# An encoder layer on one core: the exponentials' table and the values' scaling moved to ScalarE behind a maximum, a rotation bound to group 1, and unit products ahead of the first projection

## Chip, core and metric

The kernel runs on 1 core of one Trainium2 chip. The time is device microseconds (us) of one execution, measured on that core. The engines are TensorE (PE for its matmuls, PEld for its weight loads), VectorE (DVE), ScalarE (ACT), GpSimd (POOL) and SyncE (SP, which only issues DMAs here).

## What is computed

One encoder layer with two mixers side by side, on 1024 tokens of width 1024, all in float32. The change touches the input projection and mixer A.

```python
def reference(x, norm1_g, w_in, qa_norm_g, ka_norm_g, ...):
    tables = axial_rope_tables(s)
    hn = rms_norm(x, norm1_g)
    proj = hn @ w_in                       # 1024 x 2304: qa 512, ka 128, va 128, qb 512, kb 512, vb 512
    ...
    qa = apply_axial_rope(rms_norm(qa, qa_norm_g), tables)   # 8 heads of 64
    ka = apply_axial_rope(rms_norm(ka, ka_norm_g), tables)   # 2 heads of 64
    out_a = global_gqa_attention(qa, ka, va)                 # dense softmax over 1024 keys
    out_b = dilated_mixture_attention(rms_norm(qb, qb_norm_g), rms_norm(kb, kb_norm_g), vb)
    mixed = jnp.concatenate([rms_norm(out_a, outa_norm_g), rms_norm(out_b, outb_norm_g)], axis=-1)
    x = x + mixed @ w_out
    return x + conv_ffn(rms_norm(x, norm2_g), w_up, conv_w, conv_b, w_down)
```

## The kernel before

**Arithmetic.** A float32 operand is kept as two parts, high and low, and a product is three matmuls (high x high, high x low, low x high). ACT makes the high part with a copy, DVE or POOL the low part with a subtraction (`split`, lines 231 to 233; `kv_split` for the key and value weights, 270 to 273).

**Stages.** Tokens come in 8 tiles of 128. First, tile by tile, `x_prep(tt)` transposes the tokens on PE (line 180) and splits them, `x_rest(tt)` takes the sum of squares for the norm on ACT (`Square`, line 248, with a read-out instruction) and copies the transposed tokens out of PSUM (line 252, and 254 to 258 for tiles 4 to 7), `kv_proj(tt)` computes keys and values of mixer A (lines 283 to 285, 24 matmuls), and `kv_out(tt)` copies them out (line 295) and sends them to memory. Then come 28 block products (`in_product`, lines 408 to 410; `in_out`, line 420, empties a product's bank on DVE), seven for each of four chunks kb, vb, qa, qb of the weights; `w_scale` (367) and `w_prep` (381 to 392) scale, combine and split the weights. The first products stand in the code between the tiles' projections.

**Around the last products.** `k_ready(u)` transposes the rotated keys and copies them to SBUF twice on ACT (336, 337). `v_scale` multiplies the values by the norm of their token on DVE (348). Line 1062 is an exponential of one element with scale 0, there to load the table of the exponentials on ACT. `load_v` (699) fetches values of mixer B from memory; `v_split` makes their high part on ACT (709).

**Mixer A** is 16 groups g: query tiles b = g // 2 and key head kv = g % 2. `a_prep(g)` makes the queries: split (613, 614), transposes and a copy on ACT (`first`, 629), four maxima over all keys (`mx`, two matmuls 634 and two DVE reductions 635 each) and `last` (638, 642). `a_main(g)` runs 8 key tiles: scores (661, 662), exponential on ACT (664), product with the values (656) two tiles later; beside them it takes the next group's `a_prep` by the table `plan` and deferred steps by the table `late_plan`. `o_norm` (681, 682) divides.

**Rotation.** Norm and rotation of the queries are lists of steps (`done`). Those of the last query product are not done at once but `deferred`: the steps from the third on of `deferred[0]` (query tiles 4 to 7, key head 1) and `deferred[1]` (the same tiles, key head 0) go into `late`. In them POOL multiplies by the sine part (`rot`, line 289, and 504), DVE by the cosine part and adds (511, 514). Query tiles 4 to 7 are read by the groups from 8 on.

**What sets the order.** The code is written once in program order; a scheduler of the framework then puts each engine's instructions in an order of its own, within the dependencies it sees, and sets the waits. An instruction can be held back by letting it read an element that another writes, or write one that another reads: a small copy with such operands is called a tick here. Each engine runs its instructions in order.

Of the kernel before, what the change touches and what calls it, by code (L numbers as in the profile page):

```python
# [43 lines left out]
R_K2A = 16384  # L44
# [79 lines left out]
def tile_encoder_layer(ctx, tc, x, w_in, gains, outg, norm1_g, norm2_g, w_out, w_up, conv_w, conv_b,  # L124
# [110 lines left out]
    def x_bank(tt):  # L235
        return 4 + 2 * (tt % 2)
# [8 lines left out]
    def x_rest(tt):  # L245
        q0, q1 = qab(tt % 4), qab(tt % 4 + 4)
        b = x_bank(tt), x_bank(tt) + 1
        act(f(F_JNK, 512).bitcast(BF), f(qab(tt), 1024), AF.Square, accum_out=f(SM_SS1 + tt, 1))
        vec.tensor_scalar(f(SM_E1 + tt, 1), f(SM_SS1 + tt, 1), EPS / D, EPS * EPS, op0=OP.mult, op1=OP.add)
        if tt < 4:  # L250
            for half in range(2):
                act(f(q0 + 512 * half, 512), bank(b[half]), AF.Copy)
        else:
            act(f(q1, 512), bank(b[0]), AF.Copy)
            vec.tensor_tensor(f(q1 + 512, 512), f(q0, 512), bank(b[0]), op=OP.subtract)
            vec.tensor_tensor(f(q1, 512), bank(b[1]), f(q1, 512), op=OP.add)
            gp.tensor_tensor(f(q0, 512), f(q1, 512), f(q0, 512), op=OP.subtract)
            gp.tensor_tensor(f(q0 + 512, 512), f(q0 + 512, 512), f(q0, 512), op=OP.subtract)
# [16 lines left out]
    def kv_bank(tt):  # L275
        return tt if tt < 4 else 2 + tt % 2

    def kv_proj(tt):
        for k in range(8):
            a = a_op(((1, 2), (3, 4))[tt // 4][k // 4], tt % 4) + 128 * (k % 4)  # L280
            w = R_A[7] + 2048 * (k // 4) + 256 * (k % 4)
            o = bank(kv_bank(tt), 256)
            mm(o, r(a, 128), r(w, 256), start=(k == 0), stop=False)
            mm(o, r(a, 128), r(w + 1024, 256), start=False, stop=False)
            mm(o, r(a + 512, 128), r(w, 256), start=False, stop=(k == 7))
# [57 lines left out]
                kvscr[:, :, 128 + 64 * kv:192 + 64 * kv].rearrange("t p c -> p t c"))  # L343

    def v_scale():
        for kv in range(2):
            v = fp(F_VA + 66 * kv, [132, 8], [1, 64])
            vec.tensor_tensor(v, v, f(SM_R1, 8)[:, :, None].to_broadcast([128, 8, 64]), op=OP.mult)

    def fill_k():  # L350
        for i in range(4):
# [210 lines left out]
    dma(f(qab(3), 1024), perm_rows(x, 3, D))  # L562
    w_load(0, 0)
    vec.tensor_copy(r(R_IDR, 128), f(O_IDF, 128))
    nc.tensor.transpose(bank(7, 8), f(F_CST, 128)[0:8], f(O_IDF, 8)[0:8])
    vec.tensor_copy(f(SM_G1, 8), bank(7, 8))
    x_prep(0)
    for k in range(8):
        kv_split(k)
    x_prep(1)  # L570
    dma(f(F_ROPE, 1024), rope)
    for i, o in enumerate((O_GA, O_GA + 128, O_GB, O_GB + 64)):
# [406 lines left out]

    prep = [lambda: fill(rp(R_QLN + 64, [128, 8], [1, 64]), 8, 64, 0.0, eng=act)] + a_prep(0)  # L980
    for i in range(4):
        kv_proj(i)
        x_rest(i)
        x_prep(i + 2)
        if i == 0:
            late_consts()
        kv_out(i)
        if i == 2:
            w_scale(0, 0)
            w_prep(0)  # L990
        if i == 3:
            w_scale(0, 1)
            w_prep(1)
    v, rt = f(SM_T + 96, 8), f(SM_MC + 8, 8)
    for m in range(len(prods)):
# [61 lines left out]
        if last and n == 7:  # L1057
            for u in (1, 2):
                k_ready(u)
            v_scale()  # L1060

            act(f(SM_T + 96, 1), rf(R_K2A + 512, 1), AF.Exp, scale=0.0)
        if last and n == 6:
            k_ready(3)
            take(prep, 3)
        if last and n == 3:
            take(prep, 3)
    take(prep, 99)
    assert not going
    deferred += later  # L1070
    late = last_sums + [t for d in deferred[:2] for t in done(*d, 0)[3:]]

    spread = {}
    for i, d in enumerate(deferred[2:]):
        square_at, mean_at, root_at, refine_at, norm_at, gain = done(*d, i)
        spread[5 + i, 2] = [square_at]
# [13 lines left out]
    for g in range(16):  # L1090

        prep += a_prep(g + 1) if g < 15 else []
        if g == 14:
            prep += [lambda: b_split(0)] + b_prep(0)
        tail = a_main(g, prep, tail, late, {14: (1, 1, 1, 1, 1, 2, 2, 2), 15: (2, 2, 2, 2, 1, 1, 1, 1)}.get(
            g, (1, 1, 1, 1, 1, 1, 1, 0)),
                      (0, 1, 1, 0, 1, 0, 1, 0) if g < 3 else (0, 0, 1, 0, 1, 0, 1, 0) if g < 7 else (0, 1, 0, 0, 0, 1, 0, 0))
        if g == 7:
            dma(f(F_CNT, 384), cnt)
            gp.memset(fp(F_VCN + 64, [66, 8]), 1.0)  # L1100
# [417 lines left out]
```

## Times and profile before

| | before |
|---|---|
| runs | 1340.53, 1342.11, 1344.23 us (median 1342.11) |
| profiled execution | 1342.88 us, span 1341.1 us |
| PE busy | 1310.6 us, 98% of the span |
| DVE, ACT, POOL busy | 987.8, 677.1, 361.1 us |
| mean granted PE clock | 0.998 |

PE is busy in nearly the whole span. So its idle time, and the few stretches in which its clock is granted at half, are what remains to look at; idle time of the other engines matters only where PE waits for them. In the rows below a time in brackets with an arrow is the idle time ahead of that instruction, and after the arrow stands what ended it.

### The profile page before, as it was taken

How to read it: one execution, taken by the hardware profiler on the slowest of the kernel's cores; microseconds unless marked ns; L12 is line 12 of the kernel's file. 1: busy time of each engine (PE TensorE's matmuls, PEld its weight loads, DVE VectorE, ACT ScalarE, POOL GpSimd, SP SyncE). 2: the span in 40 equal slices, each digit the busy share in tenths (PEclk: the TensorE clock that was granted, in tenths of full speed). 3: DMA queues.
4: the chain of work that ended last, by engine and by line, in shares of the span. 5: the costliest groups of instructions: out<-in, count | busy, mean ns of one | idle time of the engine just before them, and what ended most of it. 6: DMA issues, size and time to landing. Idle time of an engine off the chain costs nothing.

```text
span 1341.1 us, 20092 instructions
## 1 busy us (share of the span) xinstructions
PE 1310.6 (98%) x7559; PEld 1135.3 (85%) x7559; DVE 987.8 (74%) x1629; ACT 677.1 (50%) x1062; POOL 361.1 (27%) x274
## 2 busy tenths in 40 slices
PE   7999999999999999999999999999999999999998
PEld 7999999999999888878877788888888888888887
DVE  4987686455655888875578877887787789586664
ACT  7855563455545676764365444444444445244331
POOL 0611123000111221100014565556656651100000
PEclk9999999999999999999999999999999999999999
DMA  7145212000000243342222333232233325887973
GB/s 256 52 111 126 80 39 65 9 1 0 1 9 29 67 111 109 95 147 82 94 87 71 103 110 110 87 102 96 102 115 106 102 101 190 286 295 239 297 225 110
DMA packets 119859, 148.08 MB, mean 110 GB/s; under 512 B 50833, under 2 KB 76881, under 8 KB 119761
## 3 DMA queue, kind: packets, MB, share of 16 engines
q1 hardware_dynamic: 118609, 143.65, 33.3%
q0 software_dynamic: 1152, 3.15, 0.9%
q8 instruction: 59, 0.97, 0.3%
q14 instruction: 39, 0.32, 0.1%
HBM read 112.95 MB, written 33.82 MB: 109 GB/s over the span
## 4 chain that ended last, share of the span: by engine, by line
PE 73%; DVE 13%; ACT 6%; issue 3%; POOL 3%; DMA 1%; SPq 0%; ACTq 0%; DVEq 0%; POOLq 0%
PE ps L1223 8%; PE ps L1224 8%; PE ps L1225 8%; PE ps L656 7%; PE ps L1339 5%; PE ps L1340 5%; PE ps L1338 5%; PE ps L661 3%; PE ps L634 2%; DVE bigf L1256 2%; PE ps L662 2%; PE ps L837 2%; PE ps L904 2%; PE ps L906 2%; PE ps L905 2%
## 5 line engine op out<-in xcount | busy, mean ns | idle before, releaser
L1223 PE MATMUL ps<-bigr 128*128 128x512 f32 x616 | 241.1, 392 | 6.7 <-DVE bigf L1227 6.1
L1224 PE MATMUL ps<-bigr 128*128 128x512 f32 x616 | 239.7, 389 | 0.0
L1225 PE MATMUL ps<-bigr 128*128 128x512 f32 x616 | 239.7, 389 | 0.0
L1206 ACT ACTIVATE bigr<-bigf 128x512 fp32r<-128x512 f32 x154 | 92.9, 625 | 159.2 <-POOL bigf L1198 95.4
L1256 DVE SCALAR_TENSOR_TENSOR bigf<-bigf 128x768 f32<-128x768 f32 (+1 forms) x176 | 146.3, 889 | 26.3 <-ACT bigf L1254 26.3
L656 PEld LDWEIGHTS ps<-bigf 128*128 128x128 f32 x1024 | 139.4, 191 | 10.4
L1223 PEld LDWEIGHTS ps<-bigr 128*128 128x128 f32 x616 | 115.6, 188 | 35.8 <-DVE bigf L1227 9.9
L1318 ACT ACTIVATE bigr<-bigf 128x1024 fp32r<-128x1024 f32 x77 | 80.7, 1060 | 119.2 <-PE ps L1340 71.3
L1207 DVE TENSOR_TENSOR bigr<-bigf,bigr 128x512 fp32r<-128x512 f32 x112 | 116.6, 1058 | 32.6 <-ACT bigr L1206 32.6
L1225 PEld LDWEIGHTS ps<-bigr 128*128 128x128 f32 x616 | 115.6, 188 | 23.9
L1224 PEld LDWEIGHTS ps<-bigr 128*128 128x128 f32 x616 | 115.7, 188 | 23.7
L656 PE MATMUL ps<-bigf 128*128 128x65 f32 x1024 | 134.3, 267 | 0.0
L408 PE MATMUL ps<-bigr 128*128 128x256 f32 x448 | 127.7, 285 | 1.2 <-ACT bigf L295 1.2
L409 PE MATMUL ps<-bigr 128*128 128x256 f32 x448 | 127.3, 284 | 0.0
L410 PE MATMUL ps<-bigr 128*128 128x256 f32 x448 | 127.1, 284 | 0.0
L664 ACT ACTIVATE bigf<-ps 128x512 f32<-128x512 f32 x128 | 76.0, 597 | 92.6 <-PE ps L662 91.5
L1338 PE MATMUL ps<-bigr 128*128 128x512 f32 x308 | 119.8, 389 | 0.0
L1339 PE MATMUL ps<-bigr 128*128 128x512 f32 x308 | 119.8, 389 | 0.0
L1340 PE MATMUL ps<-bigr 128*128 128x512 f32 x308 | 119.8, 389 | 0.0
L1319 DVE TENSOR_TENSOR bigr<-bigf,bigr 128x1024 fp32r<-128x1024 f32 x77 | 93.0, 1221 | 26.6 <-ACT bigr L1318 22.4
L635 DVE TENSOR_REDUCE bigf<-ps 128x1 f32<-128x512 f32 x128 | 86.5, 690 | 22.8 <-PE ps L634 20.9
L1270 POOL TENSOR_TENSOR bigf<-bigf 128x512 f32<-128x512 f32 x44 | 69.1, 1591 | 89.9 <-DVE bigf L1261 65.6
(228 smaller groups left out, 2889.8 us busy)
## 6 DMA issues: line engine op xcount, KB each, us to landing
bigf<-w_down SPq DMA_DIRECT2D x99, 256.0 KB, 4.4
bigf<-w_up SPq DMA_DIRECT2D x44, 512.0 KB, 4.3
bigf<-gscr SPq DMA_DIRECT2D x77, 256.0 KB, 4.0
gscr<-bigf SPq DMA_DIRECT2D x33, 512.0 KB, 2.7
bigf<-w_in SPq DMA_DIRECT2D x8, 1024.0 KB, 5.4
bigf<-x SPq DMA_DIRECT2D x15, 512.0 KB, 6.9
bigf<-tmx SPq DMA_DIRECT2D x8, 672.0 KB, 3.7
bigf<-w_out SPq DMA_DIRECT2D x8, 512.0 KB, 5.9
```

The costliest lines, as they stand in the source:

```text
L408: mm(o, ah, wh, start=(k == 0 and t % 2 == 0 and n != 2), stop=False, skip_group_check=True)
L409: mm(o, ah, wl, start=False, stop=False, skip_group_check=True)
L410: mm(o, al, wh, start=False, stop=(k == 3), skip_group_check=True)
L656: mm(bank(ob, 65, 66 * i), f(slots[kt] + 128 * i, 128), f(F_VA + 132 * kt + 66 * kv, 65), start=(kt == 0 and i == 0), stop=(kt == 7), skip ...
L1207: (gp if n in (2, 4) and m > 3 else vec).tensor_tensor(rp(o + 512, [128, 4], [1, 128]), src, rfp(o, [128, 4], [1, 128]), op=OP.subtract)
L1223: mm(bank(b), wh, th, start=(k == 0 and n in (1, 5, 6, 7)), stop=False, skip_group_check=True)
L1224: mm(bank(b), wh, tl, start=False, stop=False, skip_group_check=True)
L1225: mm(bank(b), wl, th, start=False, stop=(k == 3), skip_group_check=True)
L1256: vec.scalar_tensor_tensor(f(a + o, n), f(i + d, n), w_, f(a + o, n), op0=OP.mult, op1=OP.add)
L1338: mm(o, ah, r(d, 512), start=(q == 0 and n in (1, 5, 2)), stop=False, skip_group_check=True)
L1339: mm(o, ah, r(d + 1024, 512), start=False, stop=False, skip_group_check=True)
L1340: mm(o, al, r(d, 512), start=False, stop=(q == NQ - 1), skip_group_check=True)
```

## The change

Four things. (1) In `v_scale` the two DVE multiplications become eight ACT copies with a scale per partition, behind two small DVE copies, of which the first reads a maximum; the one-element exponential that loads the table stands behind the first queries' copy, and `v_scale` behind the maxima. (2) The steps of `deferred[1]` from the third on (`turns`) leave `late` and are given to `spread` in group 1: three at key tile 2 behind a tick, two at key tile 4, the rest at key tile 7; `late_plan` is one table for all groups. (3) Ahead of the transposes of norm_g twelve products of the unit matrix with itself go to a bank that nobody reads; behind token tile 0 follow one that reads its second half, and sixteen more. The first half of the first key and value projection stands ahead of token tile 1. (4) In `x_rest` a tick, for all tiles but the first, lets the sum of squares wait for DVE's part of the split.

```diff
     def x_rest(tt):
         q0, q1 = qab(tt % 4), qab(tt % 4 + 4)
         b = x_bank(tt), x_bank(tt) + 1
+        if tt:
+
+            vec.tensor_copy(f(F_JNK, 1), rf(a_op(((1, 2), (3, 4))[tt // 4][1], tt % 4) + 512, 1))
         act(f(F_JNK, 512).bitcast(BF), f(qab(tt), 1024), AF.Square, accum_out=f(SM_SS1 + tt, 1))
...
-    def kv_proj(tt):
-        for k in range(8):
+    def kv_proj(tt, ks=range(8)):
+        for k in ks:
...
     def v_scale():
-        for kv in range(2):
-            v = fp(F_VA + 66 * kv, [132, 8], [1, 64])
-            vec.tensor_tensor(v, v, f(SM_R1, 8)[:, :, None].to_broadcast([128, 8, 64]), op=OP.mult)
+
+        vec.tensor_copy(f(SM_SS1, 1), f(SM_MC, 1))
+        vec.tensor_copy(f(SM_SS1, 8), f(SM_R1, 8))
+        for t in range(8):
+            v = fp(F_VA + 132 * t, [66, 2], [1, 64])
+            act(v, v, AF.Copy, scale=f(SM_SS1 + t, 1))
...
     vec.tensor_copy(r(R_IDR, 128), f(O_IDF, 128))
+
+    idle = lambda n: [mm(bank(0, 128), r(R_IDR, 128), r(R_IDR, 128), start=True, stop=True) for _ in range(n)]
+    idle(12)
     nc.tensor.transpose(bank(7, 8), f(F_CST, 128)[0:8], f(O_IDF, 8)[0:8])
     vec.tensor_copy(f(SM_G1, 8), bank(7, 8))
     x_prep(0)
+
+    mm(bank(0, 128), r(R_IDR, 128), r(a_op(2, 0), 128), start=True, stop=True)
+    idle(16)
     for k in range(8):
         kv_split(k)
+    kv_proj(0, range(4))
     x_prep(1)
...
-        kv_proj(i)
+        kv_proj(i, range(0 if i else 4, 8))
...
-            v_scale()
-
-            act(f(SM_T + 96, 1), rf(R_K2A + 512, 1), AF.Exp, scale=0.0)
         if last and n == 6:
             k_ready(3)
-            take(prep, 3)
+            take(prep, 1)
+
+            act(f(SM_T + 96, 1), rf(R_Q2A, 1), AF.Exp, scale=0.0)
+            take(prep, 2)
         if last and n == 3:
             take(prep, 3)
+            v_scale()
...
-    late = last_sums + [t for d in deferred[:2] for t in done(*d, 0)[3:]]
-
-    spread = {}
+    late = last_sums + done(*deferred[0], 0)[3:]
+    turns = done(*deferred[1], 0)[3:]
+
+    spread = {(1, 2): [lambda now: vec.tensor_copy(f(F_KN[0], 1), now)] + [lambda now, t=t: t() for t in turns[:3]],
+              (1, 4): [lambda now, t=t: t() for t in turns[3:5]], (1, 7): [lambda now, t=t: t() for t in turns[5:]]}
...
-                      (0, 1, 1, 0, 1, 0, 1, 0) if g < 3 else (0, 0, 1, 0, 1, 0, 1, 0) if g < 7 else (0, 1, 0, 0, 0, 1, 0, 0))
+                      (0, 2, 2, 2, 1, 1, 1, 1))
```

The changed kernel's lines are shifted: from `x_rest` on by 3, from `v_scale` on by 6, from the start's code on by 9 to 13.

PE's first rows of the order, before. L180 is a transpose of tokens, L565 that of norm_g, L283 to L285 the first key and value projection.

```order
L180 MATMUL ps<-bigf 128x128 x8
L565 MATMUL ps<-bigf 128x8
L283 MATMUL ps<-bigr 128x256
L284 MATMUL ps<-bigr 128x256
L180 MATMUL ps<-bigf 128x128 x8
L285 MATMUL ps<-bigr 128x256
```

The same place after. L572 and L578 are the unit products, L574 is norm_g, L286 to L288 the projection.

```order
L572 MATMUL ps<-bigr 128x128 x12
L574 MATMUL ps<-bigf 128x8
L180 MATMUL ps<-bigf 128x128 x8
L578 MATMUL ps<-bigr 128x128
L572 MATMUL ps<-bigr 128x128 x16
L286 MATMUL ps<-bigr 128x256
L287 MATMUL ps<-bigr 128x256
L288 MATMUL ps<-bigr 128x256
```

The unit products stand on both sides of token tile 0's transposes, and those of tile 1, which stood behind the second matmul of the projection, now follow its twelfth.

ACT at the end of the input projection, before. L336 and L337 are the keys' copies, L1062 the exponentials' table, L391 the last split of weights, L629 and L613 queries, L709 values of mixer B, L642 the query part with the maxima.

```order
L336 ACTIVATE bigr<-ps 128x2x2x128
L337 ACTIVATE bigr<-ps 64x2x2x128
L1062 ACT_TABLE_LOAD
L1062 ACTIVATE bigf<-bigr 128x1
L391 ACTIVATE bigr<-bigf 128x1024
L336 ACTIVATE bigr<-ps 128x2x2x128
L337 ACTIVATE bigr<-ps 64x2x2x128
L629 ACTIVATE bigr<-ps 128x512
L613 ACTIVATE bigr<-bigf 128x512
L709 ACTIVATE bigr<-bigf 128x8x64
L642 ACTIVATE bigr<-ps 128x512
```

The same place after. L339 and L340 are the keys' copies, L397 the split of weights, L722 the values of mixer B, L642 and L626 queries, L1077 the table, L354 the values' scaling.

```order
L339 ACTIVATE bigr<-ps 128x2x2x128
L340 ACTIVATE bigr<-ps 64x2x2x128
L397 ACTIVATE bigr<-bigf 128x1024
L722 ACTIVATE bigr<-bigf 128x8x64
L339 ACTIVATE bigr<-ps 128x2x2x128
L340 ACTIVATE bigr<-ps 64x2x2x128
L642 ACTIVATE bigr<-ps 128x512
L626 ACTIVATE bigr<-bigf 128x512
L1077 ACT_TABLE_LOAD
L1077 ACTIVATE bigf<-bigr 128x1
L354 ACTIVATE bigf<-bigf 128x2x64 x8
```

The table moved behind the queries, the scaling came in behind it, and the copy of mixer B's values moved from behind the queries to ahead of the last keys.

DVE from the last maxima of group 0's stretch to those of group 1's, before. L635 is a maximum, L638 joins the halves, L511 and L514 end a rotation, L614 is a query's low part, L681 and L682 are the division.

```order
L635 TENSOR_REDUCE bigf<-ps 128x1 x8
L511 TENSOR_TENSOR bigf<-bigf 128x4x256
L638 TENSOR_TENSOR bigr<-bigf 128x4
L514 TENSOR_TENSOR bigf<-bigf 128x4x256
L614 TENSOR_TENSOR bigr<-bigf,bigr 128x4x64
L511 TENSOR_TENSOR bigf<-bigf 128x4x256
L681 RECIPROCAL bigf<-ps 128x4
L514 TENSOR_TENSOR bigf<-bigf 128x4x256
L635 TENSOR_REDUCE bigf<-ps 128x1 x2
L682 TENSOR_TENSOR bigf<-ps,bigf 128x256
L635 TENSOR_REDUCE bigf<-ps 128x1 x6
L638 TENSOR_TENSOR bigr<-bigf 128x4
```

The same place after. L648 is a maximum, L651 joins, L517 and L520 end a rotation, L627 is the low part, L694 and L695 the division, L1088 the tick.

```order
L648 TENSOR_REDUCE bigf<-ps 128x1 x8
L517 TENSOR_TENSOR bigf<-bigf 128x4x256
L651 TENSOR_TENSOR bigr<-bigf 128x4
L520 TENSOR_TENSOR bigf<-bigf 128x4x256
L627 TENSOR_TENSOR bigr<-bigf,bigr 128x4x64
L694 RECIPROCAL bigf<-ps 128x4
L695 TENSOR_TENSOR bigf<-ps,bigf 128x256
L1088 COPY bigf<-bigf 128x1
L648 TENSOR_REDUCE bigf<-ps 128x1 x8
L517 TENSOR_TENSOR bigf<-bigf 128x4x256
L651 TENSOR_TENSOR bigr<-bigf 128x4
L520 TENSOR_TENSOR bigf<-bigf 128x4x256
```

The second pair that ends a rotation moved from ahead of group 1's maxima to behind the last of them.

## Rows read from the trace of the kernel before

**Rows 1.** The page's part 1: busy us, share of span, instructions by engine.

```profile
PE 1310.6 (98%) x7559; PEld 1135.3 (85%) x7559; DVE 987.8 (74%) x1629; ACT 677.1 (50%) x1062; POOL 361.1 (27%) x274
```

**Rows 2.** PE's timeline: start, duration, engine, line, operation, count, idle time before and releaser.

```profile
4.46 1.94 PE L180 MATMUL ps<-bigf 128*128 128x128 f32 x8 [4.46 <-DMA bigf<-x]
...
9.10 0.58 PE L283 MATMUL ps<-bigr 128*128 128x256 f32 x1 [2.51 <-ACT bigr L272]
...
198.41 0.70 PE L634 MATMUL ps<-bigr 128*128 128x512 f32 x2 [1.85 <-ACT bigr L709]
...
232.57 0.50 PE L634 MATMUL ps<-bigr 128*128 128x512 f32 x1 [0.79 <-DVE bigf L635]
...
755.71 0.50 PE L1223 MATMUL ps<-bigr 128*128 128x512 f32 x1 [1.22 <-DVE bigf L1227]
```

**Rows 3.** Waits from 0 to 60 us: engine, line, releaser, total us, times, longest.

```profile
PE ps L408 <- ACT bigf L295: 1.2, 2, 0.6
```

**Rows 4.** Windows: length, busy us (instructions) of PE, PEld, DVE, ACT, POOL; granted clock, DMA.

```profile
15.04:28.80 13.76, 13.74 (x115) 13.29 (x113) 5.71 (x17) 12.00 (x24) 3.12 (x2) 1.00 0.83 305
28.80:58.00 29.20, 28.03 (x235) 27.62 (x234) 27.04 (x35) 25.95 (x47) 19.33 (x11) 1.00 0.06 20
58.00:196.50 138.50, 138.50 (x1159) 138.36 (x1159) 110.98 (x144) 82.40 (x119) 24.59 (x27) 1.00 0.32 87
...
199.36:202.78 3.42, 3.42 (x15) 3.06 (x15) 2.54 (x5) 0.00 (x0) 1.33 (x1) 0.50 0.93 350
202.78:212.50 9.72, 9.72 (x80) 9.54 (x80) 5.63 (x9) 0.60 (x1) 1.28 (x2) 1.00 0.21 56
755.80:759.20 3.40, 3.40 (x15) 2.82 (x16) 2.37 (x3) 1.15 (x2) 2.77 (x3) 1.00 0.81 258
```

**Rows 5.** PE's timeline in the first projection, one matmul on either side of 15.04.

```profile
14.48 0.41 PE L285 MATMUL ps<-bigr 128*128 128x256 f32 x1
...
15.45 0.28 PE L284 MATMUL ps<-bigr 128*128 128x256 f32 x1
```

**Rows 6.** ACT's timeline at the start.

```profile
8.54 1.70 ACT L272 ACTIVATE bigr<-bigf 128x256 fp32r<-128x256 f32 x4 [1.52 <-DMA bigf<-w_in]
10.15 1.04 ACT L248 ACTIVATE bigf<-bigf 128x1024 bf16<-128x1024 f32 x1
...
16.72 0.39 ACT L295 ACTIVATE bigf<-ps 128x256 f32<-128x256 f32 x1 [1.91 <-PE ps L285]
```

**Rows 7.** DVE's groups by form, 16 to 40 us: count, busy us, mean ns, idle before.

```profile
L249 DVE TENSOR_SCALAR bigf<-bigf 128x1 f32<-128x1 f32 x5 | 0.8, 150 | 4.4 <-ACT bigf L248 4.4
```

**Rows 8.** DVE's timeline at the end of the input projection.

```profile
190.16 1.28 DVE L348 TENSOR_TENSOR bigf<-bigf 128x512 f32<-128x512 f32 x2
...
192.50 1.21 DVE L392 TENSOR_TENSOR bigr<-bigf,bigr 128x1024 fp32r<-128x1024 f32 x1
...
197.05 1.22 DVE L420 TENSOR_TENSOR bigf<-ps,bigf 128x1024 f32<-128x1024 f32 x1
```

**Rows 9.** SP's queue at the same place: the issue of mixer B's values.

```profile
193.75 0.83 SPq L699 DMA_DIRECT2D bigf<-vscr  x2
```

**Rows 10.** DMA from 196 to 198 us: busy tenths in 40 slices of 0.05 us.

```profile
DMA  6654323688645331000000000000000000000000
```

**Rows 11.** ACT's timeline at the end of the input projection.

```profile
193.42 1.28 ACT L1062 ACT_TABLE_LOAD   x1
...
195.78 0.58 ACT L336 ACTIVATE bigr<-ps 128x512 fp32r<-128x512 f32 x1
...
197.73 0.63 ACT L709 ACTIVATE bigr<-bigf 128x512 fp32r<-128x512 f32 x1
```

**Rows 12.** POOL's timeline in group 1: the rotation's products.

```profile
225.98 3.41 POOL L289 TENSOR_TENSOR bigf<-bigf 128x128 f32<-128x128 f32 x8
```

**Rows 13.** DVE's timeline in group 1.

```profile
229.43 1.23 DVE L511 TENSOR_TENSOR bigf<-bigf 128x1024 f32<-128x1024 f32 x1 [3.28 <-POOL bigf L289]
...
231.83 1.28 DVE L635 TENSOR_REDUCE bigf<-ps 128x1 f32<-128x512 f32 x2
```

## The prediction

> **What bounds the kernel now.** I read the page's busy times first: TensorE (PE) is busy 1310.6 of 1341.1 us [rows 1]. So only about 30 us are to be had in the whole kernel, and a change that touches only the first 240 us can win what PE idles there, or what PE does slowly. Next comes PE's timeline, for what stands in brackets behind a matmul: the idle time in front of it and who ended it [rows 2]. PE waits 4.46 us for the first tokens; then 2.51 us at 9.10 for the first split of the key and value weights by ScalarE (ACT); later 1.85 us at 198.41, where the input projection ends and group 0 begins; and 0.79 us at 232.57 in group 1. Two more gaps, 1.2 us together, near 54 and 57 us are in the view of waits, ended by ACT's copies of the key and value projection [rows 3]. The windows tell the rest [rows 4]: from 58.0 to 196.5 PE is busy 138.50 of 138.50 us, with DVE at 110.98 and ACT at 82.40, so nothing that is won ahead of 58 us is eaten there by an engine that is full; and in 199.36 to 202.78, right behind the 1.85 us gap, the granted clock is 0.50. Last, the clock at the start: a 128x256 matmul takes 0.41 us at 14.48 and 0.28 us at 15.45 [rows 5], so PE starts at its lower level (1.2 GHz) and rises to 2.4 GHz at about 15 us.
>
> All working is against the profiled execution, 1342.88 us (1341.1 of span and 1.8 around it). The median of the three runs is 1342.11, 0.77 lower; I don't correct for that.
>
> **The start.** The change adds 29 unit products and one transposition order. Twelve products run as soon as the identity is there, inside the 4.46 us in which PE waits for tokens [rows 2], so they cost nothing. One more waits for ACT's second copy of token tile 0, and sixteen follow it. ACT was done with that copy at 8.54 - 1.52 = 7.02 [rows 6]. The sum of squares of tile 0, which now stands first on ACT, takes 1.04 and about 0.2 for its read-out [rows 6]; it can begin when the tokens land, before the first copy could, so about 0.6 of it is in front of the copies and the gated product starts at 7.6. A unit product has no row at this clock. The eight transposes at 4.46, of the same 128x128 shape, take 1.94 us, at most 0.24 each [rows 2]; half of that is the other bound, 0.12. Seventeen take 2.0 to 4.1 us; I take 0.16 each, a little under the middle, so 2.7 us, and the first key/value matmul moves from 9.10 to about 10.4 (9.6 to 11.7). That is a loss of 1.3 us at that place. Against it stands the clock. PE had worked 1.94 us, idled 2.51 and then worked without a gap from 9.10 until the rise [rows 2, 5]. With products filling 2.9 to 10.4 nearly without a gap I take the rise 3 us earlier, at about 12. Bounds: none earlier (15), and 4.46 earlier (10.5), the idle time that the products fill.
>
> What this is worth is set by ACT. It stands idle 1.91 us until 16.72, where PE ends the projection of token tile 0 [rows 6]; from then on it is full: 12.00 us busy in the 13.76 from 15.04 on, and 1.68 of the missing 1.76 are that one wait [rows 4]. Its lateness is what later makes PE wait the 1.2 us [rows 3]. In the new order the sum of squares (1.23) no longer stands between the two halves of the weight split, and all twelve matmuls of the first half stand together ahead of token tile 1's transposes. I get the end of that projection at 14.7 instead of 16.7, of which ACT can use 1.9. Against it, ACT's sums of squares of tiles 1 to 7 now wait for a one-element DVE copy behind the split of the same tile. Such a copy costs 0.15 on DVE, like the one-element operations there now [rows 7]; DVE is busy only 5.71 of 13.76 us in this stretch [rows 4], so seven cost it nothing. ACT's wait at the first I put at 0.2 to 0.5, and the later ones at nothing since the split is done while ACT copies. Term: -1.9 + 0.2 = **-1.7 us**. PE's two gaps are a consequence of the same lateness, so they are in it and not added. Bounds: 0 (the rise is no earlier) and -3.1 (1.9 and the whole 1.2).
>
> **The transition from projection to group 0.** Now DVE spends 1.28 us at 190.16 on the two scalings of the values, in front of L387 and L392, which ends at 193.71 [rows 8]. The loads of the second mixer's values are issued at 193.75, right behind it [rows 9], and land when the DMA digits go to zero, after 16 of 40 slices of 0.05 us in 196 to 198, at 196.8 [rows 10]: 3.1 us after L392. ACT spends 1.28 on a table load at 193.42, then the split of the weights, the last key copies at 195.78, the query copies, and the value copy at 197.73 [rows 11]. PE's gap is put down to that value copy, but it had just begun when PE went on; DVE's L420, which empties the product's bank from 197.05 to 198.27, is what ends last [rows 2, 8].
>
> The change replaces the two scalings by two tiny DVE copies behind the second query part's maximum, and eight ACT copies behind the table load, all after the transition. DVE's L387 and L392 come about 1.2 earlier, the weight split on ACT 1.4 earlier, L420 about 1.3 earlier, ending at 197.0 or before. The value loads land at 195.6. But the value copy now stands ahead of the last key copies and of the query copy that PE waits for. Starts there are 0.48 apart (195.78 to 197.73 hold four) [rows 11]: value copy 195.7, keys 196.2 and 196.7, query 197.1 to 197.7. PE goes on at 197.8 instead of 198.41: **-0.6 us**. Bounds: 0, if the loads land no earlier, and -1.85, the whole gap.
>
> The eight ACT copies have no row. Weight splits of twice the size take 1.70 for four, 0.43 each [rows 6], so at most 3.4 and with the table load 4.7. What hides them is ACT's idle time: 0.00 busy in 199.36 to 202.78 and 0.60 in the 9.72 after it [rows 4]. Values are needed only in group 0, behind 212.5. Nothing is added. If that cover were gone they would cost what DVE paid, 1.28.
>
> The Trainium skill, "ScalarE: Activation LUTs", section "Rules for kernel authors", says that a multiplication belongs on VectorE and not on ScalarE. By it the scalings would stay where they are and the sum would lose this -0.6 and the next term, 1340.4. The rows disagree with it for this place: it is ACT that is idle and DVE that is waited for.
>
> **The clock behind the gap.** At 0.50 the 3.42 us do the work of 1.71 [rows 4]. It follows the gap of 1.85. The gap of 1.22 at 755.71 is followed by a window at 1.00 [rows 2, 4]. With PE back at 197.8 this gap is 1.2 us long. So I take the stretch as gone: **-1.7 us**. Bounds: 0 and -1.7.
>
> **Group 1.** There the second rotation's sum waits 3.28 us for the eight rotation products of POOL, from 225.98 for 3.41 [rows 12], and its two DVE operations stand ahead of the first maxima, which start at 231.83 [rows 13] and free the bank for which PE waits 0.79 [rows 2]. The order behind puts these two after the group's last maximum. The rotation belongs to query tiles 4 to 7, which are read first in group 8, so its lateness costs nothing. One new one-element DVE copy (0.15) ties POOL's work to group 1; what is behind it is the maxima, by 0.15 and not on the path. Term **-0.8 us**. Bounds: 0 and -1.0.
>
> Sum: 1342.88 - 1.7 - 0.6 - 1.7 - 0.8 = 1338.1; with the terms unrounded (1.7, 0.64, 1.71, 0.79) it is **1338.0**.
>
> **The rivals.**
> - The clock falls all the same (chance 0.16). One gap of each length is thin evidence. Sum without that term: 1339.8. For it: this gap stays 1.2 us long and the maxima behind it come with stalls. Against it: 755.71 [rows 2, 4]. The Trainium skill, "TensorE: Matmul & The Clock Gate", section "What's actually happening", says that the clock's watch runs freely and isn't reset when a kernel starts, so the moment of a change differs between runs; the trace, one execution, can't show it. By that page some runs would have the stretch and others not, at 1338.1 or 1339.8.
> - The value copy blocks (0.09). It waits for a DMA with the key and query copies queued behind it on ACT. If the loads land at 196.8 as now, the query copy ends at 198.8, PE idles over 2 us and the clock falls: +0.5 instead of -0.6 and nothing from the clock, 1340.9. Against it: the loads hang on L392, and DVE is free of the scalings.
> - The products don't bring the rise forward (0.13). Then the first matmul is 1.3 late and the start wins 0: 1339.8. For it: the transposes' and products' share of PE's time up to 10 us is still broken by waits.
> - The slower side (0.06): ACT's sums of squares wait at each of the seven ticks behind a full DVE operation of 1.21 [rows 8]. From 28.80 to 58.00 DVE is busy 27.04 of 29.20 us [rows 4]. Seven such waits are 8.5 us on a full ACT; the start's term becomes -1.9 + 8.5 = +6.6 and the time 1346.4. It loses more than the other terms win (3.1) from a mean wait of (1.9 + 3.1) / 7 = 0.7 us a tick. Against it: 5.71 of 13.76 in the stretch where five of them are.
>
> **How the numbers follow.** The forecast has the other 0.56. A measurement here can tell about 0.3% from no change, 4.0 us: faster means under 1338.1, slower over 1346.1. The forecast lies at that line against the median, and at -0.36% against the profiled run's own time, and its sizes scatter to both sides (start -0 to -3.1, transition -0.6 to -1.85): 0.46 of it faster, 0.10 same. The three rivals between 1339.8 and 1340.9 are same, 0.38. The last splits into 0.04 slower and 0.02 same. Faster 0.46, same 0.50, slower 0.04. The likeliest time stays the forecast's. Its own range is 1335.4 (start -3.1, transition -1.85 in place of their values) to 1339.0 (half of the start's term); the range with the rivals up to 1340.9 and not the slow side is 1335.4 to 1341.0.
>
> **What would show it.** Right: matmuls of 0.28 us from about 12 us on; ACT's first key/value copy near 14.8 and no wait of PE for such copies near 54 and 57; PE's gap near 196 at 1.2 us or less and no stretch at 0.50 behind it; no wait for the maxima in group 1. Wrong: ACT waiting for DVE at the sums of squares for over 0.5 us each; a value copy that starts later than 196; a clock that rises at 15 as before.

## The result: slower by 0.2%

The changed kernel takes 1345.12 us (median of 20 runs, 1342.80 to 1347.03) against 1342.28 us of the kernel before (20 runs beside them). The ratio is 1.0021, 95% interval [1.0014, 1.0028]: 2.8 us slower, where 1338.0 was forecast, with a range from 1335.4 to 1341.0. The profiled execution took 1346.97 us at a mean granted clock of 0.997; 7 of the 20 runs are like it (1345.70 to 1347.03), the others have 0.998 to 1.0 and 1342.80 to 1345.60, so an account of this one execution comes to more than the median's 2.8 us.

The page's part 1 of the changed kernel (busy us, share of span, instructions):

```profile
PE 1317.3 (98%) x7588; PEld 1142.6 (85%) x7588; DVE 988.1 (73%) x1637; ACT 679.1 (50%) x1070; POOL 359.9 (27%) x274
```

PE is busy 6.7 us longer than in [rows 1]: more work at half clock and the products. PE's timeline of the changed kernel, at the places of [rows 2, 5] (start, duration, line, idle before and releaser):

```profile
2.97 2.82 PE L572 MATMUL ps<-bigr 128*128 128x128 f32 x12 [2.97 <-DVE bigr L570]
...
5.93 1.97 PE L180 MATMUL ps<-bigf 128*128 128x128 f32 x8
8.58 0.47 PE L578 MATMUL ps<-bigr 128*128 128x128 f32 x1 [0.69 <-ACT bigr L232]
8.85 3.62 PE L572 MATMUL ps<-bigr 128*128 128x128 f32 x16
12.27 0.52 PE L286 MATMUL ps<-bigr 128*128 128x256 f32 x1
...
16.86 0.41 PE L287 MATMUL ps<-bigr 128*128 128x256 f32 x1
...
17.25 0.28 PE L286 MATMUL ps<-bigr 128*128 128x256 f32 x1
...
61.41 0.47 PE L414 MATMUL ps<-bigr 128*128 128x256 f32 x1 [2.40 <-ACT bigf L298]
...
203.80 0.73 PE L647 MATMUL ps<-bigr 128*128 128x512 f32 x2 [2.21 <-ACT bigr L642]
```

The first projection matmul comes at 12.27 (before 9.10), matmuls of 0.28 us from 17.25 (before about 15). The two short gaps of [rows 3] became one of 2.40 us, and the gap at the end of the projection grew from 1.85 to 2.21. Against the same matmuls of before (57.88 and 198.41) PE is 3.5 us late at 61.41 and 5.4 late at 203.80. Counted off matmul by matmul, it is 2.4 late at the end of the token tiles (54.70 against 52.28), 5.0 behind the half-clock stretch at 61.4 that was not there before, 5.4 behind the transition, and 4.4 behind group 1 (260.08 against 255.68): group 1 gives 1.0 back. The windows (length, busy us of PE, PEld, DVE, ACT, POOL; then granted clock):

```profile
61.40:64.80 3.40, 3.39 (x16) 3.40 (x17) 3.40 (x2) 3.38 (x5) 2.97 (x2) 0.52 0.25 58
64.80:68.20 3.40, 3.40 (x30) 3.40 (x29) 3.40 (x9) 0.75 (x1) 0.00 (x0) 0.97 0.82 289
205.00:208.40 3.40, 3.40 (x15) 3.12 (x15) 2.49 (x6) 0.77 (x2) 0.00 (x0) 0.51 0.75 229
```

In the first window 16 matmuls stand where the next one of the same length holds 30, and PE's lateness grows by 1.5 us over it (3.5 to 5.0). The stretch at 205 was there before as well [rows 4], the one at 61.4 is new.

### The profile page after: what moved, and what is told of

Its sections match the earlier page's. It is cut to its first block, busy times and chain, and to the rows that moved or that the text cites. A ratio compares the mean times of both kernels' runs of the same rounds, so it can differ in the third digit from the quotient of the medians.

```text
span 1345.2 us, 20169 instructions
## 1 busy us (share of the span) xinstructions
PE 1317.3 (98%) x7588; PEld 1142.6 (85%) x7588; DVE 988.1 (73%) x1637; ACT 679.1 (50%) x1070; POOL 359.9 (27%) x274
## 4 chain that ended last, share of the span: by engine, by line
PE 79%; DVE 9%; ACT 6%; issue 3%; DMA 2%; POOL 1%; SPq 0%; ACTq 0%; DVEq 0%; POOLq 0%
PE ps L1239 10%; PE ps L1240 9%; PE ps L1241 9%; PE ps L669 8%; PE ps L1355 5%; PE ps L1356 5%; PE ps L1354 5%; PE ps L674 3%; PE ps L647 2%; PE ps L675 2%; PE ps L850 2%; PE ps L917 2%; PE ps L919 2%; PE ps L918 2%; PE ps L177 1%
## 5 line engine op out<-in xcount | busy, mean ns | idle before, releaser
L669 PEld LDWEIGHTS ps<-bigf 128*128 128x128 f32 x1024 | 139.5, 191 | 10.4
L648 DVE TENSOR_REDUCE bigf<-ps 128x1 f32<-128x512 f32 x128 | 86.6, 690 | 23.9 <-PE ps L647 21.9
```

The source lines that it names most:

```text
L669: mm(bank(ob, 65, 66 * i), f(slots[kt] + 128 * i, 128), f(F_VA + 132 * kt + 66 * kv, 65), start=(kt == 0 and i == 0), stop=(kt == 7), skip ...
```

## Experiments

All ratios are to the kernel before, measured beside it, with an interval of 0.0009 to either side for most (0.0013 at most); 0.001 is 1.34 us. A difference of two ratios is uncertain by about 0.0013. Rise, gaps and rows are those of one profiled execution each. The rise is the start of the first matmul or transpose of full-speed length; the column of the granted clock doesn't show it, for it reads 1.00 from 9.10 to 15.04 in the kernel before, where the matmuls take 0.41 us.

| kernel | ratio | rise of the clock, us | PE's gap near 50 to 62 | gap at the projection's end |
|---|---|---|---|---|
| changed kernel | 1.0021 | 17.2 | 2.40 | 2.21 |
| e1_no_units | 1.0000 | 14.3 | 2.32 | 1.61 |
| e14_first12 | 1.0008 | 16.2 | 2.18 | 1.49 |
| e2_early_table | 1.0020 | 15.1 | 2.40 | 1.46 |
| e19_wide_in_change | 1.0007 | 12.2 | 2.40 | 1.51 |
| e7_no_ticks | 1.0023 | 16.5 | 2.97 | 1.63 |
| e20_change_hold | 1.0013 | 17.6 | 2.42 | 0.28 |
| e4_group1_only | 0.9989 | 14.3 | 0.63 and 0.53 | 1.84 |
| e3_old_start | 0.9988 | 14.7 | 0.62 and 0.53 | 2.16 |
| e5_hold_v | 0.9979 | 12.8 | 0.64 and 0.54 | 0.42 |
| e13_ticks_only | 0.9992 | 13.0 | 2.16 | 0.42 |
| e10_half_hold | 0.9986 | 12.9 | 2.39 | 0.42 |
| e16_table_hold | 0.9988 | 14.2 | 2.46 | under 0.35 |
| e17_wide_first | 0.9968 | 8.4 at the latest, at half again 10.6 to 13.7 | 0.54 | 0.51 |
| e11_wide, e18_wide_again | 0.9970, 0.9956 | 12.5, 6.1 | 0.55, 0.54 | 0.68, 0.46 |

### The start: the unit products

**e1_no_units** takes the 29 products out of the changed kernel.

```diff
-    idle(12)
...
-    mm(bank(0, 128), r(R_IDR, 128), r(a_op(2, 0), 128), start=True, stop=True)
-    idle(16)
```

> The changed kernel without the 29 unit products (and without the one that waits for token tile 0); all else as changed. Theory A (the products lose the start: they cost 0.21 us each and don't bring the clock's rise forward): first projection matmul near 9.1 us instead of 12.3, matmuls of 0.28 us from about 15 instead of 17.2, PE's gap of 2.4 us near 61 under 1 us and no half clock behind it; 1340.5 to 1342. Rival B (the one-element copies ahead of ACT's sums of squares and the new order of the first projection lose it): the gap near 60 stays over 1.5 us, 1344 to 1345.

Ratio 1.0000 [0.9991, 1.0009]: the products cost 0.0021, or 2.8 us, all that the change lost. But rival B was right in part: the gap of 2.3 us stays without them, with a stretch at half clock behind it (0.56 from 55.1 to 59.0), so something else makes that.

**e14_first12** keeps the first twelve and drops the rest.

```diff
-    mm(bank(0, 128), r(R_IDR, 128), r(a_op(2, 0), 128), start=True, stop=True)
-    idle(16)
```

> The changed kernel without the product that waits for ACT and the sixteen behind it; the twelve in the wait for the first tokens stay, and the first table load stays with the sum of squares. Theory A (only the products that stand ahead of the projection cost, at 0.21 us each, and the first twelve are free): first projection matmul at 8.5 to 9.5 us, 2 to 3 us under the changed kernel, 1342 to 1343. Rival (any order in which the sum of squares and its table load come first on ACT loses as much): first matmul past 10 us, 1344 to 1345.

Ratio 1.0008 [0.9999, 1.0017], 1343.3 us, between theory and rival; 0.0008 more than e1_no_units is not clear of the uncertainty. In the trace the first twelve are not free. PE's timeline of e14_first12:

```profile
2.82 2.82 PE L572 MATMUL ps<-bigr 128*128 128x128 f32 x12 [2.82 <-DVE bigr L570]
5.57 0.27 PE L574 MATMUL ps<-bigf 8*128 8x8 f32 x1
5.77 1.97 PE L180 MATMUL ps<-bigf 128*128 128x128 f32 x8
10.12 0.69 PE L180 MATMUL ps<-bigf 128*128 128x128 f32 x2 [2.39 <-DMA bigf<-x]
10.46 0.56 PE L286 MATMUL ps<-bigr 128*128 128x256 f32 x1
```

Twelve take till 5.6, and the tokens' transposes, which stood at 4.46 in [rows 2], wait for them. The first projection matmul at 10.46 is behind token tile 1's transposes and their DMA, an order of this kernel alone.

**e2_early_table** frees the first table load of ACT.

```diff
+    gp.memset(f(F_JNK + 1, 1), 0.0)
+    act(f(F_JNK + 2, 1), f(F_JNK + 1, 1), AF.Copy)
     dma(f(O_IDF, 128), ident)
```

> The changed kernel with a one-element ACT copy as its first ACT instruction, so that the first table load waits for nothing and no longer stands behind the tokens' DMA with the sum of squares. Theory A: the load's 1.28 us at 5.08 are part of the lateness; the product that waits for ACT starts near 7.3 instead of 8.6, the first projection matmul near 11.0, and the time falls by 1.0 to 1.3 us, or by up to 3 if the gap near 61 gets short enough for the clock to hold. Rival: the clock's rise sets the start whatever ACT does; it stays at 17.2 us and the time within 0.5 us of the changed kernel's 1345.1.

In the changed kernel the sum of squares is ACT's first instruction, so the load of its table waits with it for the tokens. ACT's timeline of the changed kernel:

```profile
5.08 1.28 ACT L251 ACT_TABLE_LOAD   x1 [5.08 <-DMA bigf<-x]
...
18.52 0.38 ACT L298 ACTIVATE bigf<-ps 128x256 f32<-128x256 f32 x1 [1.04 <-PE ps L288]
```

Before, the load ran ahead of all data. The edit moves it there, and the time stays, 1.0020 against 1.0021; the first projection matmul comes at 12.21 instead of 12.27. The rival holds for the time: the late transposes of the tokens hide the load. It doesn't for the rise, which was to stay at 17.2. PE's timeline of e2_early_table has the second tile's transposes already at full speed, where those of the changed kernel (at 14.94) take 1.91 us:

```profile
14.88 1.15 PE L180 MATMUL ps<-bigf 128*128 128x128 f32 x8
```

So the rise came at 15.1 with the same products, and the time was no better for it.

**e19_wide_in_change** changes only the products' shape: six and eight of 128x512 for twelve and sixteen of 128x128.

```diff
-    idle = lambda n: [mm(bank(0, 128), r(R_IDR, 128), r(R_IDR, 128), start=True, stop=True) for _ in range(n)]
-    idle(12)
+    idr4 = r(R_IDR, 128)[:, None, :].to_broadcast([128, 4, 128])
+    idle = lambda n: [mm(bank(0), r(R_IDR, 128), idr4, start=True, stop=True) for _ in range(n)]
+    idle(6)
...
-    idle(16)
+    idle(8)
```

> The changed kernel with its unit products in another shape and nothing else: six of 128x512 in place of twelve of 128x128, eight in place of sixteen. A cold 128x512 product takes 0.5 us here, so PE is busy with them at least as long as with the old ones until the rise. Theory A (the shape decides whether they bring the rise forward): rise at 9 to 13 us in place of 17.2, first projection matmul at 10 to 12, 1 to 3 us under the changed kernel. Rival (the rest of the changed start keeps it late): rise past 14 us, within 0.7 us of the changed kernel or over it.

Ratio 1.0007 [0.9998, 1.0016], 1.9 us less than the changed kernel (just clear of the uncertainty), with the products as long as before. PE's timeline of e19_wide_in_change:

```profile
8.91 3.41 PE L573 MATMUL ps<-bigr 128*128 128x512 f32 x8
12.16 0.28 PE L286 MATMUL ps<-bigr 128*128 128x256 f32 x1
```

Here the first projection matmul already takes 0.28 us; in the changed kernel, after as many microseconds of products, it takes 0.52, and the rise comes 5.0 us later. In the three other kernels with all 29 narrow products it came at 15.1 (e2), 16.5 (e7) and 17.6 (e20): the moment scatters by 2.5 us, but the earliest is 2.9 behind e19's. At the end of the token tiles (52.28 before) these four are 1.4 to 2.6 us late, e19 is 0.1. The later gaps don't explain it: e2 has the same two (2.40 and 1.46, against 2.40 and 1.51) and stays at 1.0020. So at equal length the shape of the products changed when the rise came.

### The start: the one-element copies and the order of the first projection

**e13_ticks_only** and **e10_half_hold** each add one part of the change to e5_hold_v (below).

```diff
+        if tt:
+            vec.tensor_copy(f(F_JNK, 1), rf(a_op(((1, 2), (3, 4))[tt // 4][1], tt % 4) + 512, 1))
```

> e5_hold_v with one part of the change added: the one-element DVE copies for which ACT's sums of squares of tiles 1 to 7 wait. Theory A (they made PE's gap of 2.3 us at 52.8 in e1_no_units and of 2.4 at 59 in the changed kernel): a gap of over 1.5 us in 52 to 62, 1.5 to 3 us over e5_hold_v. Rival (the first projection in two pieces makes it): within 0.5 us of e5_hold_v, gaps 0.6 and 0.5 as before.

```diff
+    kv_proj(0, range(4))
     x_prep(1)
...
-        kv_proj(i)
+        kv_proj(i, range(0 if i else 4, 8))
```

> e5_hold_v with another part of the change added: the first half of the first key and value projection ahead of token tile 1. If that order makes the gap: over 1.5 us in 52 to 62 and 1.5 to 3 us over e5_hold_v. If the one-element copies make it: within 0.5 us of e5_hold_v, or up to 1 us faster by the matmuls standing together.

Both expected that one of the two would make the long gap and the other not. Each makes it alone: 2.16 us in e13, 2.39 in e10, in place of 0.64 and 0.54. The cost is 0.0013 (1.7 us, about as large as its uncertainty; all but two of e13's runs lie above 1339.66, the highest of e5's) for the ticks and 0.0007 (0.9 us, not clear of it) for the order. How the ticks do it, the view of waits of e13_ticks_only for ACT from 40 to 56 us shows (releaser, total, times, longest):

```profile
ACT bigr L232 <- POOL bigf L260: 2.0, 2, 1.3
ACT bigf L251 <- DVE bigf L250: 0.9, 1, 0.9
ACT bigr L232 <- DVE bigf L259: 0.5, 1, 0.5
```

ACT waits for a tick only once, 0.9 us, at tile 7. But with it the copies of that tile out of PSUM come later on ACT, the two DVE steps behind them (L258, L259) get behind splits of 1.2 to 1.5 us, and POOL after those. ACT then stands before a split, waiting for POOL, with the projection's copy L298 queued behind, for which PE waits.

The order of the first projection does it another way, as ACT's timelines of e5_hold_v (two rows) and e10_half_hold show:

```profile
52.63 0.36 ACT L295 ACTIVATE bigf<-ps 128x256 f32<-128x256 f32 x1
53.81 1.02 ACT L430 ACTIVATE bigf<-ps 128x1024 f32<-128x1024 f32 x1 [0.81 <-DVE bigr L233]
...
53.22 1.02 ACT L430 ACTIVATE bigf<-ps 128x1024 f32<-128x1024 f32 x1 [1.09 <-DVE bigr L233]
54.14 0.38 ACT L295 ACTIVATE bigf<-ps 128x256 f32<-128x256 f32 x1
```

In e10 the scheduler put the copy L430 of a product's bank, which waits 1.09 us for DVE, ahead of the projection's copy L295 for which PE waits.

**e7_no_ticks** takes the ticks out of the changed kernel (the first diff of this part, undone).

> The changed kernel without the one-element DVE copies ahead of ACT's sums of squares. If they cost in it what they cost in e13_ticks_only: 1.3 to 1.8 us under the changed kernel, PE's gap of 2.4 us near 60 under 1.5. If the late start hides them: within 0.6 us of the changed kernel, the gap still over 2 us.

Ratio 1.0023: no gain. The rival holds: with the late start the gap is there without the ticks as well (2.97 us).

### Group 1 and the transition

**e4_group1_only** is the kernel before with the `late`, `turns`, `spread` and `late_plan` lines of the change; **e3_old_start** adds `v_scale` and the table's place.

> The kernel of before with the second rotation bound to group 1 alone. If the group's gain is real and stays: 1.0 to 1.2 us less than before, 1341.1, with no gap ahead of the maxima near 232. If it is given back later (POOL or DVE late in groups 2 to 4): 1342.3, gap gone but another one behind it.

> The kernel of before with two parts of the change: values' scaling and exponentials' table moved on ACT, second rotation bound to group 1. Start as before (no products, no one-element copies ahead of the sums of squares, first projection in one piece). Theory A (the copy of mixer B's values waits for its DMA ahead of the keys and the query copy): PE's gap near 197 stays 1.8 to 2.4 us with the half clock behind it, group 1 wins 1.0 to 1.2; 1341 to 1342. Rival (at the old start's pace the loads land in time): gap 1.2 us, no half clock, 1338.5.

Group 1 alone gives 0.9989 [0.9981, 0.9998], 1.5 us; in e4's profile PE gains 1.0 us in group 1, and 0.7 at the start, where nothing was changed. No gap over 0.3 us stands between 200 and 300 us any more. The parts on ACT add nothing, 0.9988: DVE is freed of 1.28 us [rows 8], but the gap grows from 1.84 to 2.16. ACT's timeline of e3_old_start shows what stands in it:

```profile
196.19 0.63 ACT L712 ACTIVATE bigr<-bigf 128x512 fp32r<-128x512 f32 x1 [1.58 <-PE ps L412]
196.73 0.58 ACT L336 ACTIVATE bigr<-ps 128x512 fp32r<-128x512 f32 x1
197.21 0.58 ACT L337 ACTIVATE bigr<-ps 64x512 fp32r<-64x512 f32 x1
197.68 0.58 ACT L632 ACTIVATE bigr<-ps 128x512 fp32r<-128x512 f32 x1
```

L712 is the value copy. The bracket names PE, but the copy waits for its loads, as its row in e2_early_table, with the same order on ACT, says:

```profile
199.64 0.63 ACT L724 ACTIVATE bigr<-bigf 128x512 fp32r<-128x512 f32 x1 [1.63 <-DMA bigf<-vscr]
```

In the changed kernel the same copy (L722) starts at 201.68, and SP's queue there shows the loads' issue at 198.25, right behind DVE's split:

```profile
198.25 1.82 SPq L712 DMA_DIRECT2D bigf<-vscr  x4
```

DMA from 199 to 203 us in the changed kernel (40 slices of 0.1 us) falls silent after 22 of them, at 201.2, 0.5 us before the copy starts:

```profile
DMA  0027952258823684347962000000000009970591
```

How much this costs PE depends on how far DVE's split is ahead. Against the same product of PE it ends 0.5 us earlier than before in the profiles of the changed kernel and e3, and PE's gap is 2.2 us with the half clock behind it. In e1, e2, e7, e14 and e19, with the same order here, it ends 1.1 to 1.4 us earlier, the gap is 1.46 to 1.63 us, and the clock holds. What shifts DVE by this 0.6 to 0.8 us was not followed.

**e5_hold_v** changes one operand of e3_old_start, so that this copy must stand behind the table load; **e20_change_hold** does the same to the changed kernel.

```diff
-            act(f(SM_T + 96, 1), rf(R_Q2A, 1), AF.Exp, scale=0.0)
+            act(r(R_VB, 1), rf(R_Q2A, 1), AF.Exp, scale=0.0)
```

> The kernel of e3_old_start with one operand changed: the one-element exponential that loads the table writes into the place of mixer B's values, so that their copy on ACT must stand behind it and no longer ahead of the last key copies. Theory A (the value copy's wait for its loads made PE's gap of 2.16 us near 196): the gap falls to 0.9 to 1.3 us, where DVE's emptying of the product's bank ends, the half clock behind it goes, and the time falls by 0.9 to 2.7 us, to 1337.5 to 1339. Rival (DVE or the last key copies end it all the same): gap 1.8 or more, 1340.

> The changed kernel with the one operand of e5_hold_v: the value copy held behind the table load. Theory A (the value copy's wait made PE's gap of 2.2 us and the half clock behind it): gap 0.4 to 1.0 us, no half clock, 1.2 to 3 us under the changed kernel's ratio of 1.0021. Rival (in the changed kernel the late DVE ends the gap): gap of 1.5 or more, no gain.

PE's timeline in e5_hold_v at that place:

```profile
195.81 0.47 PE L637 MATMUL ps<-bigr 128*128 128x512 f32 x1 [0.42 <-ACT bigr L616]
```

The window behind it (the column behind POOL's is the granted clock):

```profile
195.80:199.20 3.40, 3.15 (x20) 2.79 (x21) 3.38 (x5) 2.11 (x3) 1.17 (x1) 1.00 0.94 368
```

The gap falls from 2.16 to 0.42 us, further than the 0.9 to 1.3 expected, and the clock holds. e5 gives 0.9979 [0.9970, 0.9988], 1.2 us under e3; e20 gives 1.0013, 1.1 us under the changed kernel. Neither difference alone is clear of the uncertainty. The split is 1.1 and 1.2 us earlier in these two, so the operand's own part is seen against e2, e7 and e19: there PE makes up 1.7 to 1.9 us against the kernel before over the transition, in e20 2.7.

### A version that beats both

**e11_wide** puts products of 128x512 and the early table load into e5_hold_v; **e16_table_hold** is e11 without products, **e17_wide_first** has only the first four, **e18_wide_again** is e11 once more.

```diff
+    gp.memset(f(F_JNK + 1, 1), 0.0)
+    act(f(F_JNK + 2, 1), f(F_JNK + 1, 1), AF.Copy)
...
+    idr4 = r(R_IDR, 128)[:, None, :].to_broadcast([128, 4, 128])
+    idle = lambda n: [mm(bank(0), r(R_IDR, 128), idr4, start=True, stop=True) for _ in range(n)]
+    idle(4)
...
+    mm(bank(0, 128), r(R_IDR, 128), r(a_op(2, 0), 128), start=True, stop=True)
+    idle(4)
```

> e5_hold_v with unit products in another shape: 128x512 in place of 128x128, four in the wait for the first tokens and four (and the one that waits for ACT) behind the first transposes, and the early one-element ACT copy for the table. Theory A (only the products' shape was wrong: a 128x128 product takes 0.21 us here as does one of twice the columns): matmuls of 0.28 us from 10 to 13 us on, 1 to 2 us under e5_hold_v. Rival (products ahead of the projection don't bring the rise forward, whatever their shape): rise at 14 to 15 us or later, and 0 to 2 us over e5_hold_v.

> e11_wide without any product: e5_hold_v and the early one-element ACT copy. If the copy, and the orders on ACT that follow from it, gave e11_wide its 1.3 us over e5_hold_v: within 0.5 us of e18_wide_again. If the products gave it: within 0.5 us of e5_hold_v's ratio of 0.9979, 1.0 to 1.5 us over e18_wide_again.

> e11_wide with only the four 128x512 products in the wait for the first tokens. If products ahead of the projection only cost: 0.5 to 1.5 us under e18_wide_again. If those behind the first transposes bring the clock's rise forward: 0.5 to 1.5 us over it, with the rise later than there.

> e11_wide once more, beside the two it is compared with: a ratio of 0.996 to 0.998 to the kernel of before, 1337 to 1339. The moment of the clock's rise in the profile against the 12.5 us of e11_wide tells how much it moves from one execution of the same start to the next.

e11 and e18 give 0.9970 [0.9958, 0.9981] and 0.9956 [0.9943, 0.9968], 1337.8 and 1336.0 us. Without products (e16) it is 0.9988, so they are worth 2.4 to 4.3 us in this start. Part of that is the scheduler's order, for e16's has the long gap (2.46 us), the others' not. e16 lies 1.2 us over e5 and 4.3 over e18, so it bears out neither of its two expectations in full. e17, with the first four alone, gives 0.9968: as much as e11, and 1.6 us over e18, which is not clear of the uncertainty; its two expectations stay undecided. PE's timeline of e18_wide_again:

```profile
2.81 2.07 PE L572 MATMUL ps<-bigr 128*128 128x512 f32 x4 [2.81 <-DVE bigr L569]
...
7.48 1.15 PE L572 MATMUL ps<-bigr 128*128 128x512 f32 x4
```

The second four take 1.15 us in place of 2.07, and the three transposes at 6.08 take 0.55: full clock from 6.1 on. In e11's profile, the same program, the three took 0.90 and the second four 2.02 us, and the rise came at 12.5. In e17's, without the second four, PE stands idle before the projection and the clock falls again, with matmuls of 0.41 us from 10.97 to 13.1 (at little cost, by e17's ratio):

```profile
8.37 0.38 PE L283 MATMUL ps<-bigr 128*128 128x256 f32 x1 [1.22 <-ACT bigr L272]
...
10.97 0.41 PE L284 MATMUL ps<-bigr 128*128 128x256 f32 x1
```

## Why the prediction was wrong, step by step

**The start failed at its first step**: "with products filling 2.9 to 10.4 nearly without a gap I take the rise 3 us earlier". A PE that is busy was taken for a PE that raises its clock. Nothing in the trace of before showed such a product at this clock. The rise came 2 us later instead, and in no kernel with these products ahead of the 15.0 of before (15.1 to 17.6); the first projection matmul was 3.2 us late. e19, with wide products over the same time, had the rise at 12.2. The rival that the rise stays (0.13) held, but it was priced at nothing: with no rise to pay for it, a first matmul that is late delays ACT's copy as well, and PE was 2.4 us late at the end of the token tiles.

**The products' price** was bounded rightly and taken wrongly. The bounds were 0.12 to 0.24, the value 0.16, and they take 0.21 each (sixteen from 8.85 to 12.27), no less than a 128x256 matmul at that clock. At that price twelve are 2.6 us and don't fit between 2.97 and 4.46, so they weren't free: the transposes went from 4.46 to 5.93. Even at 0.16 they are 1.9. That sum could have been made from the bounds.

**ACT's gain of 1.9 us** was to come from the early end of token tile 0's projection. ACT's copy of it came 1.8 us later instead, 18.52 against 16.72 [rows 6].

**The ticks** were put at 0.2 to 0.5 for the first and nothing for the rest, and the slower rival had them all wait behind DVE, from a mean of 0.7 us on. Neither was it in e13: one wait of 0.9 us at one tile, and through the order of three engines a gap of 2.2. The ticks cost 1.7 us on the old start and, by e7, nothing on the changed one, where the gap stands without them. The new order of the projection was put at no cost at all; in e10 it makes the gap by swapping two copies on ACT. What failed is that a wait was priced on the waiting engine alone.

**The transition** went the way of a rival to which 0.09 was given, the value copy ahead of the keys, and by its price: PE's gap grew. The loads landed 3.0 us behind DVE's split, as taken, but the copy started 0.5 us after that, and the split, at 198.22, was only about 0.5 us earlier against PE than in [rows 8], not 1.2. The copy then held the queries back. In five other kernels the split did come 1.1 to 1.4 us earlier, and the gap was 1.46 to 1.63, not far over the 1.2 that was forecast: the step had its mechanism, but no margin for the wait of a copy that stands ahead of the queries.

**The clock behind the gap.** The term needed a gap of 1.2 us and got 2.21, so the stretch at half clock stayed; its mechanism holds where the gap is short, as e5 and e20 show. What was missed is that the start could make a second gap of that kind: behind the new one of 2.40 us PE lost 1.5 us at half clock at 61.4. The worth of the term was read from one execution, too. Of the 109 runs of the kernel before that stand beside the experiments, 26 have a mean granted clock of 1.0, which leaves no room for a stretch of 3.4 us at 0.50, so its median held less than the full 1.7 to win.

**Group 1** was right: 0.8 forecast with a bound of 1.0, 1.0 in the trace and 1.5 by e4 (0.3 to 2.5). DVE's maxima at 234.55 in the changed kernel run as soon as PE gives them, with no wait for POOL as in [rows 13]:

```profile
234.55 2.07 DVE L648 TENSOR_REDUCE bigf<-ps 128x1 f32<-128x512 f32 x3 [0.82 <-PE ps L647]
...
241.09 1.22 DVE L517 TENSOR_TENSOR bigf<-bigf 128x1024 f32<-128x1024 f32 x1
```

**The values' scaling on ACT** costs nothing there: eight copies take 2.46 us in the trace, inside the bound of 3.4. By the Trainium skill, "ScalarE: Activation LUTs", section "Rules for kernel authors", the multiplication belongs on VectorE. The trace agrees on the price (2.46 us against 1.28 on DVE [rows 8]); in the kernel's time the runs decide for neither side: e3 equals e4, and e5, with the value copy held, is 1.3 us under e4, which is not clear of the uncertainty.

By ratios, the parts are: group 1 -1.5 us, ACT's part +0.0, the ticks and the new order with the gap between +0.9 and +1.7, the products +2.8. They make 2.2 to 3.0, and 2.8 was measured; each part is uncertain by over 1 us, so the agreement is looser than it looks. The ticks and the order can't be added up, since each makes the same gap.

Open is what makes the scheduler choose these orders, and why products of 128x128 and of 128x512 that fill the same time were followed by so different rises: the runs show that they were, not by what mechanism.

## What to carry to other kernels

Filler work for PE's clock has to be tried in the shape of the real work, and timed: here narrow products only delayed the start, while wide ones won, with or without a gap behind them. An instruction that waits for a DMA must not get ahead of copies that PE needs on an in-order engine, and one operand is enough to hold it back. A wait is priced by what then queues behind it on the other engines, not by its own length. And a stretch at half clock that one profile shows is not in every run: the granted clock of each run tells how often it comes.

## What the runs showed of the hardware

- The same start has its rise at different moments: 14.7 us in e3 and 12.8 in e5, 12.5 in e11 and 6.1 in e18. The Trainium skill, "TensorE: Matmul & The Clock Gate", section "What's actually happening", says that the clock's watch isn't reset when a kernel starts, so that the moment varies. The runs agree that it varies, but by 1.9 and 6.4 us between executions here, where the page states about half a microsecond to either side.
- Not every long gap brings the half clock. Behind PE's gaps of 1.84 to 2.97 us it came in ten of the profiles (before and, twice, the changed kernel among them; 6.8 us long in e7, 3.4 in the others), and in e13 (2.16), e10 (2.39) and e2 (2.40) it did not; behind the gaps of 1.46 to 1.63 us in the table it never came. In e17 a gap of 1.22 us at the start, just behind the rise, was followed by it.
- An fp32r product of 128x128 takes 0.21 us at the lower clock, from start to start, as one of 128x256 does (changed kernel: sixteen from 8.85 to 12.27, and the matmuls from 12.59 on).
